# Phasor table, scans and log-decay sums of an S5 and gated-linear-attention mixer

## The chip, the cores and the metric

The kernel runs on one core of a Trainium2 chip, in one launch. The metric is the device time of an execution in microseconds (us). A core has TensorE (matrix products; PE in the rows), VectorE (DVE), ScalarE (ACT), GpSimd (POOL) and SyncE (SP), which here issues the DMAs. Each engine takes its instructions in order and waits on semaphores for the others.

## The reference

A two-layer encoder over 512 tokens of width 1024, float32. The first layer's mixer is what the change touches. Its input projection feeds two branches:

```python
# S5, 32 groups of 16 channels, 64 complex states, both directions
a = exp(lam_re*dt) * (cos(lam_im*dt) + i sin(lam_im*dt))
x = u @ Bbar ; h[t] = a*h[t-1] + x[t]           # reverse for direction 1
y = Re(C h) + D u ; y = gelu(y) ; y = y*sigmoid(y @ glu_w + glu_b)

# GLA, 4 heads, both directions, chunks of 64 tokens
log_a = log_sigmoid(lr @ gate_w + gate_b) / 16
bc = cumsum(log_a within a chunk) ; b_last = bc[:, :, -1]
qd, kd, kc = q*exp(bc), k*exp(-bc), k*exp(b_last - bc)
o = (mask * (qd kd^T)) v + qd S_prev ; S = S*exp(b_last) + kc^T v
```

The branches are concatenated, projected, added and normalized, and a mixture of experts follows. The second layer has windowed attention with a sink logit per head, and again a mixture of experts.

## The kernel before

The S5 branch works in chunks of 8 tokens: products with precomputed matrices do what lies inside a chunk, and a scan goes over the 64 chunks. There are four blocks, two halves of the groups (`hf`) by two directions (`d`); I call them first to fourth in their order of work (first half forward and backward, then second half). A block has:

- `s5_cs`: the phasor table `CS` on GpSimd, powers 0 to 63 of the phase of `a` for 16 groups of states, by doubling: each of five rounds squares the phase (line 653 on the tile `ph`, 128x16) and multiplies the known part of the table by it (six operations). The tag `cs` has two buffers, so the third table waits until the first block has been worked off.
- `s5_x`: the chunk inputs come from TensorE through ScalarE's copies `xb` (709, 710) and are turned by the table on VectorE (722 to 724). Since the phase is taken out, the scan's factor is the real magnitude in `eph`: 16 scans of 128x64 in line 728.
- `s5_back`: TensorE swaps real and imaginary rows (`swap`), VectorE turns the phase back (741 to 743).
- `s5_table` builds `PB` and `Mo` (611 to 613, on VectorE but for the last block's `Mo`, on GpSimd).

Per half, `s5_hs` transposes `HT` on TensorE; ScalarE copies it to `Hs` (760); SyncE writes it to DRAM (`E`) and reads it back as `Mi` with eight DMAs, and `s5_y` forms the output from `Mi`, `Mo` and `XS`, with the gelu in `yg` (791). In SyncE's queue there follow `snk` (the sink logits for the second layer), the router's small weights, four `x` loads and `glw`, the weight of the GLU, which ScalarE rounds to `glh` (801).

In the GLA branch (`gla_a`), heads lie along the free dimension and both directions' 64 features on the partitions. The gate comes from TensorE; the log-sigmoid is min(z,0) minus log(1+exp(-|z|)) (871 to 875). Then eight scans of 64x512, with a factor that is 0 where a chunk begins (879, 880), give the sums within chunks; `bl` (884, 885) is a chunk's last sum; three exponentials on ScalarE (891, 894, 895) and three products (897; two of them on GpSimd) give `kc`, `q2` and `kd`. `gla_b` transposes `kc` to `kcp` (920) and steps the states `St` (934, 938: 56 steps of 64x128 on VectorE), then forms the output.

After the GLU, `mixer0_out` loads the output weight `wo` in two DMAs (988), and the expert weights follow in SyncE's queue (1219).

GpSimd keeps the order of the program. The order of the other engines in the first mixer is set at build time by a scheduler that simulates the program, so that a changed operation moves others.

Of the kernel before, what the change touches and what calls it, by code (L numbers as in the profile page):

```python
# [108 lines left out]
class Net:  # L109
# [64 lines left out]
    def mixer0(self, A, B1):  # L174
# [160 lines left out]
        def lowrank():  # L335
# [311 lines left out]
    def s5_cs(self, d, hf):  # L647

        G, a8 = self.nc.gpsimd, self.a8
        g0 = 32 * d + 16 * hf  # L650

        def tt(o, x, y, op):
            G.tensor_tensor(o, x, y, op=op)
        CS = a8([2, 16, 64], f"CS{d}{hf}", "cs")
        self.CS[d, hf] = CS
        c, s = CS[:, 0], CS[:, 1]
        pc, psn = self.eph[:, 0, g0:g0 + 16], self.eph[:, 1, g0:g0 + 16]
        G.tensor_copy(c[:, :, 1:2], pc[:, :, None])
        G.memset(c[:, :, 0:1], 1.0)
        G.memset(s[:, :, 0:1], 0.0)  # L660
        G.tensor_copy(s[:, :, 1:2], psn[:, :, None])
        ph = a8([23, 16], "ph", "ph")
        tb = a8([16, 32], "phb", "phb")
        cur = (pc, psn)
        m = 2
        while m < 64:
            q = 2 * (m.bit_length() % 2)
            nr, ni = ph[:, q], ph[:, q + 1]

            tt(nr, cur[0], cur[0], OP.mult)  # L670
            tt(ph[:, 4], cur[1], cur[1], OP.mult)
            tt(nr, nr, ph[:, 4], OP.subtract)
            tt(ni, cur[0], cur[1], OP.mult)
            tt(ni, ni, ni, OP.add)
            cur = (nr, ni)
            bs = [128, 16, m]
            mc, ms = (t[:, :, None].to_broadcast(bs) for t in cur)
            t_ = tb[:, :, :m]
            tt(c[:, :, m:2 * m], c[:, :, :m], mc, OP.mult)
            tt(t_, s[:, :, :m], ms, OP.mult)  # L680
            tt(c[:, :, m:2 * m], c[:, :, m:2 * m], t_, OP.subtract)
            tt(s[:, :, m:2 * m], s[:, :, :m], mc, OP.mult)
            tt(t_, c[:, :, :m], ms, OP.mult)
            tt(s[:, :, m:2 * m], s[:, :, m:2 * m], t_, OP.add)
# [143 lines left out]
    def gla_a(self, qk, lrT):  # L828
# [7 lines left out]
        def tile8(name, tag):  # L836
            return self.a8([4, 512], name, tag)
        gt4 = tile8("gt4", "wl")
        WG = gt4[:, 0].rearrange("p (h d e) -> p h d e", h=4, d=2)
        rs = gt4[:, 2]  # L840
        V.memset(WG, 0.0)
        gb = self.small([4], "gb")
        for d in range(2):
# [2 lines left out]
            nc.sync.dma_start(gb[64 * d:64 * d + 64], i["gla_gate_b"][0, d].rearrange("(h e) -> e h", h=4))
        V.memset(rs, 1.0)
        V.memset(rs[0:64].rearrange("p (n c) -> p n c", c=64)[:, :, 0:1], 0.0)
        V.memset(rs[64:128].rearrange("p (n c) -> p n c", c=64)[:, :, 63:64], 0.0)
# [18 lines left out]
        for h in range(4):
            b = self.bank("p")
            self.mm(b, WG[:, h].rearrange("p d e -> p (d e)"), lrT)  # L870
            V.tensor_scalar(la[:, h], b, gb[:, h:h + 1], 0.0, op0=OP.add, op1=OP.min)
            S.activation(lt[:, h], b, AF.Abs, bias=gb[:, h:h + 1])
# [9 lines left out]
        bl = self.small([32], "bl")
        bcv = bc.rearrange("p h (n c) -> p (h n) c", c=64)
        V.tensor_copy(bl[0:64, :, None], bcv[0:64, :, 63:64])
        V.tensor_copy(bl[64:128, :, None], bcv[64:128, :, 0:1])
        dec = self.small([32], "dec", z=5)
        kc = la
        V.tensor_tensor(kc.rearrange("p h (n c) -> p (h n) c", c=64), bl[:, :, None].to_broadcast([128, 32, 64]), bcv,
                        op=OP.subtract)
        S.activation(dec, bl, AF.Exp, scale=1.0 / 16)  # L890
        S.activation(kc, kc, AF.Exp, scale=1.0 / 16)
        kd = tile8("kd", "wh")
        eb = kd
        S.activation(eb, bc, AF.Exp, scale=1.0 / 16)
        S.activation(bc, bc, AF.Exp, scale=-1.0 / 16)
        for nm, o, x, y in (("kc", kc, kc, k2), ("q2", q2, q2, eb), ("kd", kd, k2, bc)):
            (G if nm in ("q2", "kd") else V).tensor_tensor(o, x, y, op=OP.mult)
# [1194 lines left out]
```

## Time and profile before

| | us |
|---|---|
| median of 3 runs (1600.93 to 1603.47) | 1601.02 |
| profiled execution | 1606.41 |
| its span, first to last instruction | 1604.6 |
| PE busy in the span | 1388.4 (87%) |
| DVE busy | 694.6 (43%) |
| ACT busy | 355.6 (22%) |
| POOL busy (385 instructions) | 317.1 (20%) |

The busy shares are means over the whole program, of which the first mixer is the first fifth; the rest is mostly TensorE and weight traffic. So the rows below are by stage. In them a start is counted from the start of the span, and what stands in brackets is the idle time of the engine before the instruction, with what ended it.

### The profile page before, as it was taken

Reading aid. Unit: us, or ns where it says so; the run is one execution under the profiler, and the core shown is the slowest. Engines: PE = TensorE matmul, PEld = TensorE weight load, DVE = VectorE, ACT = ScalarE, POOL = GpSimd, SP = SyncE. Lnnn points to the kernel's source line nnn. Section 1 sums busy time; section 2 is a strip of 40 time slices with the busy share of each in tenths; the row PEclk is TensorE's granted clock in tenths of the full one; section 3 lists DMA queues with packets and bytes.
Section 4 is the critical chain, followed back from the end, with each engine's and each line's share of the span. In section 5 each row is a group of like instructions: output and inputs, shape, how many; then the busy total and the mean of one; then the engine's idle time right before and its main releaser. Section 6 shows DMA issues by size and latency. Waiting matters only on the chain.

```text
span 1604.6 us, 20785 instructions
## 1 busy us (share of the span) xinstructions
PE 1388.4 (87%) x8043; PEld 803.8 (50%) x8043; DVE 694.6 (43%) x1409; ACT 355.6 (22%) x643; POOL 317.1 (20%) x385
## 2 busy tenths in 40 slices
PE   6889726798997999988878898998997999989785
PEld 5778615577552435524324785667342553524242
DVE  8947997556132132311214557865231222311115
ACT  2233612331110101101002366641110110101012
POOL 5996932323000000000001434112000000000003
PEclk9999957798999999999989999998999999999998
DMA  8223006426599999999999116356899999999993
GB/s 183 67 80 86 16 20 184 156 110 240 228 407 423 423 423 424 422 420 423 420 421 358 47 60 186 115 220 242 357 407 422 422 425 422 423 421 422 422 416 132
DMA packets 122695, 461.07 MB, mean 287 GB/s; under 512 B 34650, under 2 KB 60730, under 8 KB 79968
## 3 DMA queue, kind: packets, MB, share of 16 engines
q1 hardware_dynamic: 122480, 459.59, 73.3%
q8 instruction: 65, 1.06, 0.3%
q14 instruction: 38, 0.31, 0.1%
q0 software_dynamic: 112, 0.10, 0.0%
HBM read 454.94 MB, written 4.72 MB: 286 GB/s over the span
## 4 chain that ended last, share of the span: by engine, by line
PE 49%; DMA 24%; DVE 3%; POOL 1%; issue 1%; ACT 1%; SPq 0%; POOLq 0%; ACTq 0%; DVEq 0%
PE b L119 47%; DMA w<-in_moe_w_dram 23%; PE b L133 1%; PE b L1943 1%; DVE x L1085 1%; DVE x L1120 0%; DMA cwo<-in_c_w_out_dram 0%; DVE x L1101 0%; POOL lnmv L1109 0%; DMA bias<-Ld 0%; POOL lnmv L1110 0%; DVE scv L1937 0%; DVE scv L1920 0%; POOL x L1118 0%; POOL lnmv L1073 0%
## 5 line engine op out<-in xcount | busy, mean ns | idle before, releaser
L119 PE MATMUL b<-w,xe 128*64 128x512 f32 (+1 forms) x2144 | 393.6, 614 | 30.5 <-DMA w<-in_moe_w_dram 27.3
L119 PE MATMUL b<-w,hT 128*64 128x512 f32 (+1 forms) x1088 | 227.5, 644 | 38.9 <-DMA w<-in_moe_w_dram 36.0
L119 PEld LDWEIGHTS b<-w,xe 128*64 128x64 f32 (+1 forms) x2144 | 114.7, 127 | 278.8 <-issue 220.7
L1102 POOL TENSOR_SCALAR lnmv<-lnmv 128x1 f32<-128x1 f32 x8 | 3.2, 399 | 960.9 <-DVE x L1101 483.2
L1565 DVE TENSOR_TENSOR x<-x,b 128x512 f32<-128x512 f32 x176 | 112.2, 682 | 143.2 <-PE b L119 140.9
L119 PEld LDWEIGHTS b<-w,hT 128*64 128x64 f32 (+1 forms) x1088 | 61.3, 131 | 190.8 <-issue 111.7
L1535 DVE SCALAR_TENSOR_TENSOR yl<-b,gs,yh 128x512 fp32r<-128x512 f32 x52 | 39.0, 751 | 230.4 <-ACT yh L1534 229.9
L119 PE MATMUL b<-S,xh 128*128 128x256 f32 x448 | 112.2, 291 | 0.0
L119 PE MATMUL b<-S,xl 128*128 128x256 f32 x448 | 110.6, 288 | 0.0
L1512 DVE TENSOR_TENSOR hs<-hs,b 128x512 f32<-128x512 f32 x26 | 17.9, 688 | 202.7 <-PE b L119 202.7
L119 PEld LDWEIGHTS b<-S,xh 128*128 128x128 f32 x448 | 87.3, 195 | 10.0 <-issue 9.9
L1534 ACT ACTIVATE yh<-b,gs 128x512 fp32r<-128x512 f32 x52 | 35.8, 688 | 249.3 <-PE b L119 249.1
L119 PE MATMUL b<-yh,GT 128*128 128x512 f32 x208 | 89.2, 433 | 0.1
L119 PEld LDWEIGHTS b<-S,xl 128*128 128x128 f32 x448 | 87.3, 195 | 0.0
L119 PE MATMUL b<-yl,GT 128*128 128x512 f32 x208 | 81.7, 397 | 0.7 <-DVE yl L1535 0.6
L1520 ACT ACTIVATE hT<-b 128x512 f32<-128x512 f32 x26 | 15.5, 598 | 299.8 <-PE b L133 299.8
L119 PEld LDWEIGHTS b<-yh,GT 128*128 128x128 f32 x208 | 39.5, 190 | 46.1 <-issue 33.8
L119 PE MATMUL b<-wh,xt 128*128 128x256 f32 x384 | 55.8, 298 | 7.1 <-ACT wh L168 4.6
L1511 ACT ACTIVATE hs<-b 128x512 f32<-128x512 f32 x26 | 15.6, 599 | 192.2 <-PE b L119 192.2
L119 PEld LDWEIGHTS b<-wh,xt 128*128 128x128 f32 x384 | 51.4, 204 | 8.2 <-ACT wh L168 5.2
L119 PE MATMUL b<-xTh,spa 128*128 128x512 f32 x160 | 51.6, 393 | 0.5 <-ACT scv L1840 0.5
L1465 ACT ACTIVATE xe<-b 128x512 f32<-128x512 f32 (+1 forms) x56 | 31.8, 568 | 87.4 <-PE b L119 87.4
(411 smaller groups left out, 2245.6 us busy)
## 6 DMA issues: line engine op xcount, KB each, us to landing
w<-in_moe_w_dram SPq DMA_DIRECT2D x288, 1024.0 KB, 19.6
w<-in_moe_w_dram SPq DMA_DIRECT2D x46, 2048.0 KB, 18.8
bias<-Ld SPq DMA_DIRECT2D x32, 384.0 KB, 3.5
wr<-in_ab_w_in_dram SPq DMA_DIRECT2D x8, 1024.0 KB, 6.5
x<-in_x_dram SPq DMA_DIRECT2D x8, 512.0 KB, 6.4
wo<-in_ab_w_out_dram SPq DMA_DIRECT2D x2, 2048.0 KB, 9.3
cw<-in_c_w_in_dram SPq DMA_DIRECT2D x2, 2048.0 KB, 9.4
cwo<-in_c_w_out_dram SPq DMA_DIRECT2D x16, 256.0 KB, 5.2
```

What stands on the lines that cost most here:

```text
L119: self.nc.tensor.matmul(o, l, r, start=start, stop=stop)
L133: self.nc.tensor.transpose(o, i, self.ident[:k, :k])
L1085: V.scalar_tensor_tensor(x, x, mv[:, 2:3], gb[1][:, c], op0=OP.mult, op1=OP.add)
L1102: G.tensor_scalar(mv[:, 3:4], mv[:, 0:1], mv[:, 1:2], -1.0 / 1024, op0=OP.add, op1=OP.mult)
L1465: nc.scalar.activation(xe[:, 2 * kk:2 * kk + 2, 0:n], b.rearrange("p (j s) -> p j s", j=2)[:, :, 0:n], AF.Copy)
L1511: nc.scalar.activation(hs, b1, AF.Silu)
L1512: nc.vector.tensor_mul(hs, hs, b3)
L1520: self.nc.scalar.activation(hT, b.rearrange("p (k s) -> p k s", k=4), AF.Copy)
L1534: nc.scalar.activation(yh[:, j], b[j], AF.Copy, scale=gs)
L1535: nc.vector.scalar_tensor_tensor(yl[:, j], b[j], gs, yh[:, j].bitcast(F32), op0=OP.mult, op1=OP.subtract)
L1565: V.tensor_add(xs, xs, b)
L1943: nc.tensor.transpose(b[:, 128 * g:128 * g + 128], s[:, g, 128 * j:128 * j + 128], self.rev)
```

## The change

- The phasor table is doubled from the first power on, with both planes (real and imaginary) in one operation of 4 dimensions: 24 operations a block in place of 59. The start column is copied by ScalarE, and its two memsets are VectorE's.
- The 16 scans of a block become two of 128x512. Their factor is written by ScalarE to a PSUM bank (two operations of 128x512 a block), and VectorE zeroes it where a group begins.
- The gate is computed with tokens on the partitions, with the bias as a further row of the product. The chunk sums and the remainders to the chunk's end are 64 products of `la` with masks on TensorE, into PSUM; ScalarE takes the exponentials from there, head by head, and VectorE forms `kc`, `q2` and `kd`, head by head. The GLA scans, `bl` and the difference (888) are gone, and GpSimd has none of the products.
- The negation of `snk` goes from VectorE to GpSimd.

```diff
+            V.memset(lrT[32:33], 1.0)
...
     def s5_cs(self, d, hf):
-        G, a8 = self.nc.gpsimd, self.a8
+        G, S, a8 = self.nc.gpsimd, self.nc.scalar, self.a8
...
+        self.nc.vector.memset(CS[:, 0, :, 0:1], 1.0)
+        self.nc.vector.memset(CS[:, 1, :, 0:1], 0.0)
+        S.activation(CS[:, :, :, 1:2], self.eph[:, 0:2, g0:g0 + 16][:, :, :, None], AF.Copy)
+        tb = a8([2, 16, 31], "phb", "phb")
+        m = 1
         while m < 64:
...
+            k = min(m, 63 - m)
+            o, x, bs = CS[:, :, :, m + 1:m + k + 1], CS[:, :, :, 1:k + 1], [128, 2, 16, k]
+            c, w = (CS[:, r:r + 1, :, m:m + 1].to_broadcast(bs) for r in range(2))
+            t_ = tb[:, :, :, :k]
+            G.tensor_tensor(o, x, c, op=OP.mult)
+            G.tensor_tensor(t_, x[:, ::-1], w, op=OP.mult)
+            G.tensor_tensor(o[:, 0], o[:, 0], t_[:, 0], op=OP.subtract)
+            G.tensor_tensor(o[:, 1], o[:, 1], t_[:, 1], op=OP.add)
             m *= 2
...
-        for g in range(16):
-            x1 = XF[:, g] if d == 0 else XF[:, g, ::-1]
-            V.tensor_tensor_scan(x1, self.eph[:, 2, g0 + g:g0 + g + 1].to_broadcast([128, 64]), x1, 0.0,
-                                 op0=OP.mult, op1=OP.add)
+
+        for h in range(2):
+            mg = self.bank().rearrange("p (g n) -> p g n", g=8)
+            S.activation(mg, self.eph[:, 2, g0 + 8 * h:g0 + 8 * h + 8][:, :, None].to_broadcast([128, 8, 64]), AF.Copy)
+            V.memset(mg[:, :, z0:z0 + 1], 0.0)
+            x1, mg = XS[:, h].rearrange("p j n -> p (j n)"), mg.rearrange("p g n -> p (g n)")
+            if d:
+                x1, mg = x1[:, ::-1], mg[:, ::-1]
+            V.tensor_tensor_scan(x1, mg, x1, 0.0, op0=OP.mult, op1=OP.add)
...
+            nc.sync.dma_start(WG[32:33, :, d, :], i["gla_gate_b"][0, d].rearrange("(h e) -> h e", h=4)[None])
+
+        mk = gt4[:, 1].rearrange("p (m i) -> p m i", m=4)
+        for j, op in enumerate((OP.is_ge, OP.is_le, OP.is_lt, OP.is_gt)):
+            V.tensor_scalar(mk[:, j], self.jp, 0.0, None, op0=op)
+        V.memset(mk[0:64, :, 64:128], 0.0)
+        V.memset(mk[64:128, :, 0:64], 0.0)
...
+        zs = []
+        for t in range(4):
+            b = self.bank("p" if t < 2 else "b")
+            self.mm(b, lrT[:, 128 * t:128 * t + 128], gt4[:, 0])
+            S.activation(lt[:, t], b, AF.Abs)
+            zs.append(b)
         S.activation(lt, lt, AF.Exp, scale=-1.0)
         S.activation(lt, lt, AF.Ln, bias=1.0)
-        V.tensor_tensor(la, la, lt, op=OP.subtract)
+        for t in range(4):
+            V.scalar_tensor_tensor(la[:, t], zs[t], 0.0, lt[:, t], op0=OP.min, op1=OP.subtract)
         yield
...
+        kc, kd = lt, tile8("kd", "wh")
         for h in range(4):
...
+            bs = []
+            for m in range(2):
+                b = self.bank("p")
+                for t in range(4):
+                    for d in range(2):
+                        o = 128 * h + 64 * d
+                        self.mm(b[64 * d:64 * d + 64, 128 * t:128 * t + 128], la[:, t, o:o + 64], mk[:, 2 * m + d])
+                bs.append(b)
+            b, r = bs
+            S.activation(kd[:, h], b, AF.Exp, scale=-1.0 / 16)
+            S.activation(b, b, AF.Exp, scale=1.0 / 16)
+            S.activation(kc[:, h], r, AF.Exp, scale=1.0 / 16)
+            for d in range(2):
+                a, c = slice(64 * d, 64 * d + 64), 63 - 63 * d
+                S.activation(dec[a, 8 * h:8 * h + 8, None], b[a].rearrange("p (n c) -> p n c", c=64)[:, :, c:c + 1], AF.Copy)
+            V.tensor_tensor(kc[:, h], kc[:, h], k2[:, h], op=OP.mult)
+            V.tensor_tensor(q2[:, h], q2[:, h], b, op=OP.mult)
+            V.tensor_tensor(kd[:, h], kd[:, h], k2[:, h], op=OP.mult)
...
-        V.tensor_scalar(self.snk[:, 1], self.snk[:, 0], -1.0, None, op0=OP.mult)
+        G.tensor_scalar(self.snk[:, 1], self.snk[:, 0], -1.0, None, op0=OP.mult)
```

The order of the engines changes with it, at three places of the first mixer. On VectorE the third block's scans (728) and the fourth block's turning (722, 723) stood thus before, with the GLA's scans (879, 880) between:

```order
L724 TENSOR_TENSOR XS<-XS,xb_1927 128x4x2x63
L728 SCALAR_TENSOR_TENSOR XS<-eph,XS 128x64 x16
L875 TENSOR_TENSOR la<-la,lt 128x2048
L722 TENSOR_TENSOR XS<-b_2027,CS_1445 128x4x2x63
L723 TENSOR_TENSOR xb_2003<-b_2028,CS_1445 128x8x63
L879 SCALAR_TENSOR_TENSOR lt<-gt_1992,la 64x512
L722 TENSOR_TENSOR XS<-b_2040,CS_1445 128x4x2x63
L880 SCALAR_TENSOR_TENSOR lt<-gt_1992,la 64x512
L879 SCALAR_TENSOR_TENSOR lt<-gt_1992,la 64x512
```

Now there is, from the third block's two scans (716) to the fourth's (`b_1874` to `b_1888` are its inputs, 712 the zeroing of the factor):

```order
L707 TENSOR_TENSOR XS<-XS,xb_1780 128x4x2x63
L716 SCALAR_TENSOR_TENSOR XS<-b_1829,XS 128x512
L716 SCALAR_TENSOR_TENSOR XS<-b_1833,XS 128x512
L705 TENSOR_TENSOR XS<-b_1874,CS_1339 128x4x2x63
L706 TENSOR_TENSOR xb_1850<-b_1875,CS_1339 128x8x63
L705 TENSOR_TENSOR XS<-b_1887,CS_1339 128x4x2x63
L706 TENSOR_TENSOR xb_1851<-b_1888,CS_1339 128x8x63
L712 MEMSET b_1900 128x8
L707 TENSOR_TENSOR XS<-XS,xb_1850 128x4x2x63
L712 MEMSET b_1904 128x8
L707 TENSOR_TENSOR XS<-XS,xb_1851 128x4x2x63
L716 SCALAR_TENSOR_TENSOR XS<-b_1900,XS 128x512
```

The GLA's work no longer stands between the blocks.

On ScalarE, from the second `Hs` copy on, the kernel before has (`kcp`, `kd` and `lt` belong to the GLA, `glh` and `yg` to the end of the S5 branch):

```order
L760 ACTIVATE Hs_2123<-b_2130 128x256
L920 ACTIVATE kcp<-b_2194 128x512
L920 ACTIVATE kcp<-b_2200 128x512
L920 ACTIVATE kcp<-b_2206 128x512
L920 ACTIVATE kcp<-b_2212 128x512
L894 ACTIVATE kd<-lt 128x2048
L895 ACTIVATE lt<-lt 128x2048
L801 ACTIVATE glh<-glw 128x1024 x2
L791 ACT_TABLE_LOAD
L791 ACTIVATE yg_2320<-b_2321 128x4x8x16
L791 ACTIVATE yg_2320<-b_2347 128x4x8x16
```

The changed kernel has, from `glh` on (880 is the Exp into `kd`, 881 the one in place, 882 the one into `kc`, whose buffer is `lt`; `b_2085` and `b_2094` are the sums of head 3):

```order
L788 ACTIVATE glh<-glw 128x1024 x2
L880 ACTIVATE kd<-b_2085 128x512
L881 ACTIVATE b_2085<-b_2085 128x512
L778 ACT_TABLE_LOAD
L778 ACTIVATE yg_2243<-b_2244 128x4x8x16
L882 ACT_TABLE_LOAD
L882 ACTIVATE lt<-b_2094 128x512
L885 ACTIVATE dec<-b_2085 64x8 x2
L778 ACT_TABLE_LOAD
L778 ACTIVATE yg_2243<-b_2270 128x4x8x16
L911 ACTIVATE kcp<-b_2117 128x512
L911 ACTIVATE kcp<-b_2123 128x512
```

The `kcp` copies have moved from ahead of `glh` to behind it, and with them three exponentials and table loads between.

On TensorE, where the products with `Mi` began before:

```order
L119 MATMUL b_2224<-v,kcp 128x128
L119 MATMUL b_2225<-v,kcp 128x128
L119 MATMUL b_2248<-v,kcp 128x128 x4
L119 MATMUL b_2321<-Mi_2139,U 64x128 x2
L119 MATMUL b_2321<-Mo_1773,XS 64x128
L119 MATMUL b_2347<-Mi_2139,U 64x128 x2
L119 MATMUL b_2347<-Mo_1773,XS 64x128
```

The changed kernel has there (`gt,la` are the mask products, 8 to a bank; `b_2007` is head 0, `b_2033` and `b_2042` head 1, `b_2059` and `b_2068` head 2):

```order
L119 MATMUL b_2033<-gt_1837,la 64x128 x2
L119 MATMUL b_2244<-Mi_1977,U 64x128 x2
L119 MATMUL b_2244<-Mo_1626,XS 64x128 x2
L119 MATMUL b_2244<-Mo_1986,XS 64x128
L119 MATMUL b_2270<-Mi_1977,U 64x128 x2
L119 MATMUL b_2270<-Mo_1626,XS 64x128 x2
L119 MATMUL b_2270<-Mo_1986,XS 64x128
L119 MATMUL b_2042<-gt_1837,la 64x128 x8
L119 MATMUL b_2244<-Mo_1986,XS 64x128
L119 MATMUL b_2244<-Mi_1977,U 64x128 x2
L119 MATMUL b_2244<-Mo_1626,XS 64x128 x2
L119 MATMUL b_2244<-Mo_1986,XS 64x128 x2
```

The products of the states (`v,kcp`), which stood ahead of `Mi`, come later, and mask products of heads 1 to 3 stand behind it.

## Rows read from the trace of the kernel before

**Rows 1.** 20-us window: PE, PEld, DVE, ACT, POOL busy (count), PEclk, DMA share, GB/s.

```profile
200.00:220.00 20.00, 0.00 (x0) 0.00 (x0) 19.93 (x11) 0.00 (x0) 16.44 (x6) 0.50 0.00 0
```

**Rows 2.** List of waits, 100 to 330 us: total, times, longest.

```profile
PE b L119 <- DVE XS L728: 30.9, 1, 30.9
ACT dec L890 <- DVE bl L885: 27.0, 1, 27.0
```

**Rows 3.** VectorE's timeline: start, us, engine, line, operation, tiles [idle <-releaser].

```profile
112.62 7.82 DVE L728 TENSOR_TENSOR_SCAN XS<-eph,XS 128x64 f32<-128x64 f32 x16
...
178.59 2.06 DVE L871 TENSOR_SCALAR la<-b,gb 128x512 f32<-128x512 f32 x3
...
187.18 0.67 DVE L722 TENSOR_TENSOR XS<-b,CS 128x504 f32<-128x504 f32 x1
...
191.29 10.13 DVE L728 TENSOR_TENSOR_SCAN XS<-eph,XS 128x64 f32<-128x64 f32 x16
201.35 4.05 DVE L875 TENSOR_TENSOR la<-la,lt 128x2048 f32<-128x2048 f32 x1
...
214.47 3.21 DVE L880 TENSOR_TENSOR_SCAN lt<-gt,la 64x512 f32<-64x512 f32 x1
217.69 1.22 DVE L879 TENSOR_TENSOR_SCAN lt<-gt,la 64x512 f32<-64x512 f32 x1
...
228.53 1.56 DVE L728 TENSOR_TENSOR_SCAN XS<-eph,XS 128x64 f32<-128x64 f32 x8
...
232.81 0.68 DVE L741 TENSOR_TENSOR CS<-b,CS 128x512 f32<-128x512 f32 x1
...
246.51 4.75 DVE L1846 TENSOR_SCALAR snk<-snk 128x16 f32<-128x16 f32 x1 [4.10 <-DMA snk<-in_c_sink_dram]
...
276.74 0.34 DVE L934 SCALAR_TENSOR_TENSOR St<-St,dec,b 64x128 f32<-64x128 f32 x1
277.11 0.35 DVE L938 SCALAR_TENSOR_TENSOR St<-St,dec,b 64x128 f32<-64x128 f32 x1
```

**Rows 4.** GpSimd's timeline (same columns): second, third and fourth table, then `Mo`.

```profile
100.50 0.25 POOL L653 TENSOR_TENSOR CS<-CS,ph 128x32 f32<-128x32 f32 x1
...
115.86 1.05 POOL L653 TENSOR_TENSOR CS<-CS,ph 128x512 f32<-128x512 f32 x1
...
117.99 1.30 POOL L653 TENSOR_TENSOR CS<-CS,phb 128x512 f32<-128x512 f32 x1
...
135.50 0.21 POOL L658 COPY CS<-eph 128x16 f32<-128x16 f32 x1 [12.86 <-DVE XS L743]
...
166.43 0.22 POOL L658 COPY CS<-eph 128x16 f32<-128x16 f32 x1 [2.11 <-DVE XS L743]
...
199.27 2.00 POOL L611 TENSOR_TENSOR Mo<-C,AA 128x1024 f32<-128x1024 f32 x1
```

**Rows 5.** TensorE's timeline: first `HT` transposes, first `Mi` product, last GLU product.

```profile
121.48 0.88 PE L133 MATMUL b<-ident,HT 128*128 128x128 f32 x3 [4.97 <-DVE HT L753]
...
246.30 0.70 PE L119 MATMUL b<-Mi,U 128*64 128x128 f32 x4 [5.83 <-DMA snk<-in_c_sink_dram]
...
303.64 0.39 PE L119 MATMUL b<-glh,yTl 128*128 128x512 f32 x1
```

**Rows 6.** ScalarE's timeline: table load and Exp, second `Hs` copy, `glh`, `yg`.

```profile
188.00 1.28 ACT L873 ACT_TABLE_LOAD   x1
189.29 1.91 ACT L873 ACTIVATE lt<-lt 128x2048 f32<-128x2048 f32 x1
...
234.98 0.39 ACT L760 ACTIVATE Hs<-b 128x256 f32<-128x256 f32 x1 [0.44 <-PE b L133]
...
257.43 2.00 ACT L801 ACTIVATE glh<-glw 128x1024 fp32r<-128x1024 f32 x2 [14.64 <-DMA glw<-in_s_glu_w_dram]
...
262.52 0.60 ACT L791 ACTIVATE yg<-b 128x512 f32<-128x512 f32 x1 [1.79 <-PE b L119]
```

**Rows 7.** SyncE's queue: the issue of `glw`.

```profile
247.46 0.69 SPq L391 DMA_DIRECT2D glw<-in_s_glu_w_dram  x1
```

More of the change, by code (lines that the diff above doesn't have):

```diff
@@ L647, in s5_cs @@
     def s5_cs(self, d, hf):
-        G, a8 = self.nc.gpsimd, self.a8
+        G, S, a8 = self.nc.gpsimd, self.nc.scalar, self.a8
         g0 = 32 * d + 16 * hf
-        def tt(o, x, y, op):
-            G.tensor_tensor(o, x, y, op=op)
         CS = a8([2, 16, 64], f"CS{d}{hf}", "cs")
         self.CS[d, hf] = CS
[L656 to L665, printed above, removed]
-        while m < 64:
[L667 to L684, printed above, removed]
+        self.nc.vector.memset(CS[:, 0, :, 0:1], 1.0)
[3 more added lines that the diff above has]
+        m = 1
+        while m < 64:
+            k = min(m, 63 - m)
[6 more added lines that the diff above has]
+            G.tensor_tensor(o[:, 1], o[:, 1], t_[:, 1], op=OP.add)
             m *= 2
@@ L724, in s5_x @@
             V.tensor_tensor(xv[:, js, :, hi], xv[:, js, :, hi], tmp[:, :, :, hi], op=OP.add)
-        XF = XS.rearrange("p h j n -> p (h j) n")
-        for g in range(16):
-            x1 = XF[:, g] if d == 0 else XF[:, g, ::-1]
-            V.tensor_tensor_scan(x1, self.eph[:, 2, g0 + g:g0 + g + 1].to_broadcast([128, 64]), x1, 0.0,
-                                 op0=OP.mult, op1=OP.add)
+        for h in range(2):
[6 more added lines that the diff above has]
+            V.tensor_tensor_scan(x1, mg, x1, 0.0, op0=OP.mult, op1=OP.add)
     def s5_back(self, d, hf):
@@ L839, in gla_a @@
         WG = gt4[:, 0].rearrange("p (h d e) -> p h d e", h=4, d=2)
-        rs = gt4[:, 2]
         V.memset(WG, 0.0)
-        gb = self.small([4], "gb")
         for d in range(2):
@@ L845, in gla_a @@
             nc.sync.dma_start(WG[16 * d:16 * d + 16, :, d, :], gw)
[L846 to L849, printed above, removed]
+            nc.sync.dma_start(WG[32:33, :, d, :], i["gla_gate_b"][0, d].rearrange("(h e) -> h e", h=4)[None])
[4 more added lines that the diff above has]
+        V.memset(mk[64:128, :, 0:64], 0.0)
         yield
@@ L867, in gla_a @@
         la, lt = tile8("la", "xtA"), tile8("lt", "xtA")
[L868 to L872, printed above, removed]
+        zs = []
[4 more added lines that the diff above has]
+            zs.append(b)
@@ L873, in gla_a @@
         S.activation(lt, lt, AF.Exp, scale=-1.0)
         S.activation(lt, lt, AF.Ln, bias=1.0)
-        V.tensor_tensor(la, la, lt, op=OP.subtract)
+        for t in range(4):
+            V.scalar_tensor_tensor(la[:, t], zs[t], 0.0, lt[:, t], op0=OP.min, op1=OP.subtract)
         yield
-        bc = lt
+        dec = self.small([32], "dec", z=5)
+        kc, kd = lt, tile8("kd", "wh")
         for h in range(4):
-            V.tensor_tensor_scan(bc[0:64, h], rs[0:64], la[0:64, h], 0.0, op0=OP.mult, op1=OP.add)
-            V.tensor_tensor_scan(bc[64:128, h, ::-1], rs[64:128, ::-1], la[64:128, h, ::-1], 0.0,
-                                 op0=OP.mult, op1=OP.add)
@@ L882, in gla_a @@
[L882 to L897, printed above, removed]
+            bs = []
[6 more added lines that the diff above has]
+                bs.append(b)
```

## The prediction

> **What bounds the kernel now.** I read the chain of waits first: it cannot be followed back beyond 320 us, so the first mixer has to be read by stage. The table of 20-us windows shows the stage that matters: from 200 to 220 us TensorE does nothing at all and ScalarE does nothing, while VectorE is busy for 19.93 us with eleven instructions and GpSimd for 16.44 [rows 1]. The list of waits names the same hole twice: TensorE waits 30.9 us, once, for the S5 scans of line 728, and ScalarE 27.0 us for `bl`, which follows the GLA scans [rows 2]. Then I read VectorE's rows through that hole. Sixteen scans of 128x64 took 10.13 us beside GpSimd's phasor table; eight of the same took 1.56 with GpSimd idle. A 64x512 scan of the decays took 3.21 beside GpSimd and 1.22 alone [rows 3]. So the stage is bound by VectorE, and part of that by the company of GpSimd. Behind it the chain runs over the last S5 half (swap on TensorE, `Hs` on ScalarE, a round trip through DRAM to `Mi`), the GLA states (the `St` rows), GLU, and the copy of `wo`; from there the weight stream of the first MoE hangs on the place where SyncE gets to it, and I let every microsecond won before pass through 1:1.
>
> **S5 scans: 16 of 128x64 become 2 of 128x512.** The trace has no 128x512 scan with a multiplicand in PSUM. The nearest rows are the 64x512 scans: 1.22 alone, 3.21 beside GpSimd [rows 3]. I take 1.22: VectorE's multiplies with one operand in PSUM took 0.67 beside the table and 0.68 with GpSimd idle, so an operand from PSUM takes the contention away [rows 3]. The Trainium skill says the same ("SBUF — State Buffer", section "Who interferes with whom"): a VectorE instruction with at most one input in SBUF does not contend with GpSimd; by this rule the new scan costs 1.22 beside a table too, and without it 3.21. The trace agrees for multiplies and shows no such scan.
> A block's scans then cost 2.44 instead of 7.82, 10.13 or 3.12. In the first block TensorE idles 4.97 us at 121.48 for `HT`, which stands behind these scans on VectorE [rows 3, 5]; 7.82 - 2.44 = 5.4 covers it, so this wait goes: 5.0 us. The two multiplicands a block are written by ScalarE (0.6 us each by the `yg` row of 128x512 [rows 6]) while it waits anyway, and cost nothing; if that cover were gone, 1.2 us a block.
>
> **Phasor table: 59 GpSimd operations a block become 24.** GpSimd's multiplies took 0.25 at 32 elements, 1.05 at 512 and 2.00 at 1024; its add and subtract 1.30 at 512 [rows 4]. On a line through these, the twelve multiplies (32 to 992 elements, 1984 in each of two sets) cost 2 x (6 x 0.20 + 1984 x 0.00175) = 9.3 us, the twelve subtracts and adds (16 to 496) 2 x (6 x 0.20 + 992 x 0.00215) = 6.7: 16 a block. That is the low end; the high end is no gain, as the strided two-plane operands have no row. Now the fourth table runs from 166.43 to the start of the `Mo` work at 199.27 [rows 4], 32.8 us. Its start hangs on the buffer that the block two before frees: the third table waited 12.86 us for it [rows 4]. Both buffers come free some 5 us earlier, and the third table is shorter, so I put the fourth at 157 to 174 and the `Mo` work behind it (17.3 us now) to 189. On GpSimd nothing else waits: the gain is that the table is out of VectorE's way. ScalarE's copy of the start column stands in its queue ahead of each table; I price it at nothing, as GpSimd waits for the buffer then.
>
> **Decay sums on TensorE.** The third S5 block started at 187.18. TensorE's 5.0 carry over to it, and the bias operations of line 871 (2.06 for three, some 2.7 for four) no longer stand before it: 179.6. Its multiplies (187.18 to 191.29) cost 4.1 as before, the scans 2.4: 186.1, against 201.35. Before, the subtraction of line 875 (4.05) and the decay scans now pushed the fourth block's scans back to 230.09; now they come straight behind: 4.1 + 2.4 more, 192.6. From there to the end of the second `Hs` copy it took 5.3 (230.09 to 235.37 [rows 3, 6]). In the new order that copy stands behind a table load and an Exp on ScalarE, 1.28 + 1.91 [rows 6]: 201.1, or 34 us earlier. Then a load and Ln, and four small operations of 0.67 on VectorE, give `la` at 207.0; the 64 mask products come on a TensorE that is idle, except those that stand behind `Mi`.
>
> **What is late next.** The second `Hs` copy starts SyncE's chain E, `Mi`, the small loads and `glw`. Now `glw` was issued 12.1 us after the copy's end and landed another 9.96 later, where `glh` on ScalarE waits for it [rows 6, 7]. I keep these 22.1: `glw` lands at 223.2. This is the new wait. In the old order only `glh` and work that was not urgent stood there; in the new one the exponentials of head 3 stand behind `glh` in ScalarE's queue, and all of the `kcp` copies behind them, on which the GLA states hang. By then they wait: `Mi` came 10.9 us after the copy's end (TensorE goes on at 246.30 [rows 5]), so at 212, and the mask products of heads 1 to 3, which stand behind it on TensorE, are through by some 220. Then, with durations of rows 6: `glh` 2.0, two Exp 1.2, load 1.28, `yg` 0.6, load 1.28, Exp 0.6, the two `dec` copies some 0.5, load 1.28, `yg` 0.6, four `kcp` copies 2.1: 11.4, 234.6; the first products after them let `St` start at 235.9. Its 56 steps follow each other by 0.37 (the last two rows' spacing, [rows 3]): 20.7, with the two `gll` operations 2.3 and 1.5 for waits between: 260.5. Before, the last ended at 277.46 (277.11 + 0.35). The difference is **17 us**. That `snk` leaves VectorE's queue is inside this: there VectorE waited 4.10 us for its DMA and then spent up to 4.75 on it, among the `St` steps [rows 3].
> The Trainium skill speaks against the change here ("ScalarE: Activation LUTs", section "What ACT_TABLE_LOAD costs"): a switch of the table set is 1.28 us of load and 1.38 of drain. Here the Exp starts 0.01 us behind the end of the load at 188.00 [rows 6]: no drain is to be seen. By the page the three loads on this piece would cost 4.1 us more, and the gain would be 13.
>
> **Sum.** The profiled execution took 1606.41 us (1604.6 of span and 1.8 around it); 17 less is 1589.4. It lies 5.4 above the median of the runs, 1601.02, which I take off: **1584 us**. The forecast's own range, with waits in the ScalarE chain a few us either way, is 1577 to 1590.
>
> **Rivals.**
> *GpSimd stays slow* (0.18). Small or strided operations cost what they cost now, the fourth table takes its 32.8 us and ends at 190, `Mo` at 207, and the four late scans run beside it at 3.21. Each block is 4 us later, `Hs` 8. For it: the table's price has no row. Against: the first operands come from PSUM. Gain 9: 1592.
> *The new wait isn't there* (0.16). If `glw` lands before ScalarE gets to it, 5 us of the wait go, and a TensorE that pauses less may keep its clock: it was granted 0.50 (the 1.2 GHz level) in the idle window [rows 1], and the work behind `Mi` ran at this level; 5 more. Gain 27: 1574. Against: `glw` hangs on the same copy as `Mi`.
> *The new wait decides* (0.10): slower. In the new order `St`'s end is `Hs`'s end plus 59.4 (22.1 + 12.7 + 24.6), while the old one didn't hang on `glw`. So the change gains only if the second `Hs` copy ends before 218.1, 17.3 us earlier than now; if the banks that the fourth block borrows, or the multiplicands from ScalarE, hold the S5 blocks where they were, all of the removed work on VectorE is lost in this queue: up to 17 us slower, 1618; half as bad, 1609. For it: one queue decides. Against: ten of the 34 us are removed by scans alone, and nothing that holds the block is on the list of waits.
> *The change doesn't reach the end* (0.04): the weight stream of the first MoE is set by something earlier, 1601. Against: SyncE issues it behind `wo`, whose buffer waits for the GLU.
>
> **How the numbers follow.** Forecast 0.52, the rivals 0.18, 0.16, 0.10, 0.04. Range 1569 to 1599: forecast and the first two rivals with some room, 0.86 of the cases less what may fall outside them. Faster by over 0.2% (3.2 us, about what a measurement of this kernel can tell from no change): 0.84; within 0.2%: 0.06; slower: 0.10.
>
> **What would show it.** In the profile after: scans of 128x512 near 1.2 us even where GpSimd is busy; a GpSimd table of about 16 us; no idle of TensorE before the `HT` transposes of the first half; the second `Hs` copy near 201; `glh` still waiting for `glw`, with the exponentials of the last head behind it; no `snk` among the `St` rows; the last `St` near 260 and the last GLU product near 287 instead of 304 [rows 5]. Scans of 3 us, or a `Hs` copy later than 218, would make the forecast wrong; so would a `St` chain that starts much later than 13 us after `glw`.

## The result, and the profile after

The changed kernel takes 1625.43 us (median, 1624.78 to 1626.93), the kernel before on the same chip 1600.97: ratio 1.0153 [1.0135, 1.0171], **slower by 24 us**, where 1584 was forecast. Its profiled execution took 1625.35 us, its span 1623.6. The loss is there at the last GLU product, 19.8 us later than before; what follows is equally long (1299.8 us of span, before 1300.6). The profiled execution of the kernel before was 5.4 us slower than its median, so the two spans differ by 19.0 us only. VectorE is busy for 675.9 us and GpSimd for 273.5 (244 instructions), both less than before, and TensorE for 1410.8, more.

| us from the span's start | before | forecast | after |
|---|---|---|---|
| third block starts | 187.18 | 179.6 | 201.16 |
| second `Hs` copy ends | 235.37 | 201.1 | 222.41 |
| `glw` landed, `glh` starts | 257.43 | 223.2 | 246.78 |
| first `St` starts | 241.32 | 235.9 | 264.40 |
| last `St` ends | 277.46 | 260.5 | 292.95 |
| last GLU product ends | 304.03 | 287 | 323.85 |

The hole of [rows 1] is gone, as this window row shows (TensorE and ScalarE work in it, VectorE is not full):

```profile
200.00:220.00 20.00, 13.56 (x67) 8.93 (x68) 17.29 (x29) 6.07 (x11) 3.41 (x2) 0.74 0.01 4
```

What was lost lies on both sides of it. First, VectorE's timeline of the changed kernel: the first block's `HT`, a scan beside the third table, and the way into the third block (start, us, engine, line, operation, tiles):

```profile
118.90 2.34 DVE L716 TENSOR_TENSOR_SCAN XS<-b,XS 128x512 f32<-128x512 f32 x2
121.16 0.20 DVE L738 TENSOR_TENSOR HT<-HT 128x64 f32<-128x64 f32 x1
121.40 0.67 DVE L740 SCALAR_TENSOR_TENSOR HT<-eye,Dv,HT 128x16 f32<-128x16 f32 x4
...
146.48 2.34 DVE L716 TENSOR_TENSOR_SCAN XS<-b,XS 128x512 f32<-128x512 f32 x2
...
178.98 2.86 DVE L614 TENSOR_TENSOR PB<-PB,TPB 128x1024 f32<-128x1024 f32 x1
...
181.77 2.92 DVE L614 TENSOR_TENSOR PB<-PB,TPB 128x1024 f32<-128x1024 f32 x1
184.61 4.25 DVE L613 TENSOR_TENSOR TMo<-C,AA 128x1024 f32<-128x1024 f32 x2
...
189.92 2.04 DVE L738 TENSOR_TENSOR HT<-HT 128x64 f32<-128x64 f32 x1
191.88 3.04 DVE L614 TENSOR_TENSOR Mo<-Mo,TMo 128x1024 f32<-128x1024 f32 x1
194.85 6.39 DVE L740 SCALAR_TENSOR_TENSOR HT<-eye,Dv,HT 128x16 f32<-128x16 f32 x4
201.16 0.67 DVE L705 TENSOR_TENSOR XS<-b,CS 128x504 f32<-128x504 f32 x1
...
204.92 2.34 DVE L716 TENSOR_TENSOR_SCAN XS<-b,XS 128x512 f32<-128x512 f32 x2
```

And GpSimd's: a multiply of the third table, then the end of the fourth and the `Mo` work behind it:

```profile
146.86 1.11 POOL L664 TENSOR_TENSOR CS<-CS 128x512 f32<-128x512 f32 x1
...
178.01 2.75 POOL L664 TENSOR_TENSOR CS<-CS 128x992 f32<-128x992 f32 x1
180.73 2.88 POOL L665 TENSOR_TENSOR phb<-CS 128x992 f32<-128x992 f32 x1
183.69 2.00 POOL L666 TENSOR_TENSOR CS<-CS,phb 128x496 f32<-128x496 f32 x1
...
189.29 2.58 POOL L612 TENSOR_TENSOR Mo<-C,AA 128x1024 f32<-128x1024 f32 x1 [1.51 <-ACT xb L693]
191.84 2.00 POOL L613 TENSOR_TENSOR TMo<-C,AA 128x1024 f32<-128x1024 f32 x1
193.92 3.20 POOL L614 TENSOR_TENSOR Mo<-Mo,TMo 128x1024 f32<-128x1024 f32 x1
197.09 2.00 POOL L612 TENSOR_TENSOR Mo<-C,AA 128x1024 f32<-128x1024 f32 x1
```

The kernel before had the same two VectorE operations on `PB` in its own line 613, and the four small ones on `HT` in line 753, beside smaller operations of GpSimd:

```profile
176.31 1.20 DVE L613 TENSOR_TENSOR PB<-PB,TPB 128x1024 f32<-128x1024 f32 x1
177.44 1.23 DVE L613 TENSOR_TENSOR PB<-PB,TPB 128x1024 f32<-128x1024 f32 x1
...
185.93 0.66 DVE L753 SCALAR_TENSOR_TENSOR HT<-eye,Dv,HT 128x16 f32<-128x16 f32 x4
```

```profile
175.22 4.00 POOL L653 TENSOR_TENSOR ph<-ph 128x16 f32<-128x16 f32 x5
```

Read starts and durations of both engines against each other: a VectorE operation with two operands in SBUF and a GpSimd operation take turns, and a row's time holds the wait for the other engine. `PB` from 178.98 ends at 181.84, 1.1 us behind the GpSimd multiply that ends at 180.76; the next multiply, begun at 180.73, ends at 183.61, 1.8 behind `PB`. So a 1.2-us operation takes 2.9 beside one of 992 elements. Four operations of 16 elements, 0.67 us in all at 121.40, take 6.39 at 194.85. What these stand beside is not the table but GpSimd's `Mo` work: it is as large as before, but the table ends at 187.77 instead of 199.27, so this work has moved up beside `HT`. The scans, with an operand in PSUM, take 2.34 for two, and so they do at 146.48 beside a multiply of the third table: that step of the forecast held.

ScalarE's timeline from the second `Hs` copy to the last `kcp` ([rows 6] are those of before):

```profile
222.05 0.36 ACT L747 ACTIVATE Hs<-b 128x256 f32<-128x256 f32 x1
...
246.78 2.00 ACT L788 ACTIVATE glh<-glw 128x1024 fp32r<-128x1024 f32 x2 [4.47 <-DMA glw<-in_s_glu_w_dram]
248.80 0.60 ACT L880 ACTIVATE kd<-b 128x512 f32<-128x512 f32 x1
...
249.91 1.28 ACT L778 ACT_TABLE_LOAD   x1
...
253.11 0.60 ACT L882 ACTIVATE lt<-b 128x512 f32<-128x512 f32 x1
...
256.68 1.08 ACT L911 ACTIVATE kcp<-b 128x512 f32<-128x512 f32 x2 [0.83 <-PE b L133]
...
262.27 0.60 ACT L911 ACTIVATE kcp<-b 128x512 f32<-128x512 f32 x1 [2.59 <-PE b L133]
```

The queue is as forecast, `glh` waiting for `glw` with head 3's exponentials and all of `kcp` behind it. But the four `kcp` copies take 6.2 us instead of 2.1 (256.68 to 262.87), the last with 2.59 us of wait for its transposes, and `St` starts 17.6 us after `glh` instead of 12.7. TensorE's rows of these transposes (between them stand products `q,kd` of the GLA; the products with `Mi` are over by 246.5):

```profile
253.76 0.90 PE L133 MATMUL b<-ident,lt 128*128 128x128 f32 x3 [6.33 <-ACT lt L882]
...
258.98 2.67 PE L119 MATMUL b<-q,kd 64*128 64x128 f32 x18
261.58 0.66 PE L133 MATMUL b<-ident,lt 128*128 128x128 f32 x4
```

Then VectorE's and TensorE's timelines and the window row of the states:

```profile
264.40 0.34 DVE L925 SCALAR_TENSOR_TENSOR St<-St,dec,b 64x128 f32<-64x128 f32 x1 [1.18 <-PE b L119]
...
274.05 0.35 DVE L929 SCALAR_TENSOR_TENSOR St<-St,dec,b 64x128 f32<-64x128 f32 x1 [1.84 <-PE b L119]
...
292.60 0.35 DVE L929 SCALAR_TENSOR_TENSOR St<-St,dec,b 64x128 f32<-64x128 f32 x1
```

```profile
271.97 3.06 PE L119 MATMUL b<-v,kcp 64*128 64x128 f32 x16 [5.42 <-DVE St L925]
...
288.66 0.70 PE L119 MATMUL b<-St,q 128*64 128x128 f32 x4
...
323.46 0.39 PE L119 MATMUL b<-glh,yTl 128*128 128x512 f32 x1
```

```profile
280.00:300.00 20.00, 16.06 (x76) 10.95 (x75) 12.21 (x31) 1.36 (x11) 0.00 (x0) 0.50 0.00 1
```

TensorE and VectorE wait for each other by turns until 288 us, up to 5.42 us at a time on the one side and three times 1.84 on the other, and TensorE's granted clock in the window is 0.50, the 1.2 GHz level.

### The profile page after: what moved, and what is told of

It reads as the page before. It is cut to its first block, busy times and chain, and to the rows that moved or that the text cites. A ratio compares the mean times of both kernels' runs of the same rounds, so it can differ in the third digit from the quotient of the medians.

```text
span 1623.6 us, 20890 instructions
## 1 busy us (share of the span) xinstructions
PE 1410.8 (87%) x8171; PEld 822.8 (51%) x8171; DVE 675.9 (42%) x1371; ACT 364.9 (22%) x673; POOL 273.5 (17%) x244
## 5 line engine op out<-in xcount | busy, mean ns | idle before, releaser
L119 PE MATMUL b<-w,hT 128*64 128x512 f32 (+1 forms) x1088 | 224.0, 651 | 34.6 <-DMA w<-in_moe_w_dram 31.8
L1525 ACT ACTIVATE yh<-b,gs 128x512 fp32r<-128x512 f32 x52 | 35.7, 687 | 241.7 <-PE b L119 241.4
## 6 DMA issues: line engine op xcount, KB each, us to landing
w<-in_moe_w_dram SPq DMA_DIRECT2D x288, 1024.0 KB, 19.8
```

The lines of the kernel that those rows point to most:

```text
L119: self.nc.tensor.matmul(o, l, r, start=start, stop=stop)
L1525: nc.scalar.activation(yh[:, j], b[j], AF.Copy, scale=gs)
```

## The experiments

Shown are the marks of one profiled execution each; its own time lies up to 6 us from the median. "Rest" is the span less the last GLU product. The experiments ran on four chips (e1 to e4, e5 to e8, f, g); each ratio is to the kernel before on the same chip, where its median was 1603.27, 1601.91, 1602.51 and 1603.16. So runs of different groups are compared here by their ratios, and a difference of medians between them can be some us off.

| | median | ratio to before | `Hs` end | `St` | GLU end | rest |
|---|---|---|---|---|---|---|
| before | 1600.97 | 1 | 235.4 | 241.3 to 277.5 | 304.0 | 1300.6 |
| after | 1625.43 | 1.0153 [1.0135, 1.0171] | 222.4 | 264.4 to 293.0 | 323.9 | 1299.8 |
| e1 | 1602.96 | 1.0002 [0.9980, 1.0025] | 231.8 | 242.5 to 273.4 | 297.1 | 1299.1 |
| e2 | 1607.53 | 1.0019 [1.0005, 1.0033] | 226.8 | 239.2 to 270.9 | 301.0 | 1300.2 |
| e3 | 1622.37 | 1.0108 [1.0078, 1.0139] | 224.7 | 267.8 to 296.5 | 326.6 | 1293.2 |
| e4 | 1610.16 | 1.0029 [1.0014, 1.0044] | 214.3 | 257.3 to 286.0 | 316.2 | 1290.3 |
| e5 | 1598.42 | 0.9986 [0.9967, 1.0004] | 234.5 | 245.1 to 272.4 | 296.1 | 1300.4 |
| e6 | 1597.71 | 0.9965 [0.9948, 0.9983] | 213.2 | 244.0 to 272.6 | 303.6 | 1287.7 |
| e7 | 1612.89 | 1.0061 [1.0041, 1.0081] | 223.6 | 254.7 to 281.5 | 312.0 | 1300.2 |
| e8 | 1621.72 | 1.0108 [1.0078, 1.0138] | 218.9 | 262.4 to 291.0 | 321.3 | 1299.8 |
| f1 | 1583.19 | 0.9881 [0.9861, 0.9901] | 214.8 | 241.1 to 261.5 | 287.6 | 1292.6 |
| f2 | 1592.43 | 0.9941 [0.9924, 0.9958] | 214.6 | 241.4 to 270.0 | 301.4 | 1290.8 |
| f3 | 1581.28 | 0.9872 [0.9851, 0.9892] | 212.0 | 237.9 to 258.3 | 284.4 | 1291.1 |
| f4 | 1599.40 | 0.9975 [0.9962, 0.9988] | 223.0 | 249.3 to 269.7 | 295.8 | 1301.9 |
| g1 | 1590.28 | 0.9916 [0.9893, 0.9938] | 214.0 | 240.0 to 260.4 | 290.7 | 1297.6 |
| g2 | 1589.49 | 0.9919 [0.9892, 0.9946] | 223.1 | 249.4 to 269.8 | 295.9 | 1291.5 |
| g3 | 1597.39 | 0.9951 [0.9931, 0.9971] | 234.3 | 244.8 to 275.5 | 302.1 | 1293.5 |

**One part alone, or all but one.** These take hunks of the change's diff as they stand there: e1 is before with the new `s5_cs`, e2 before with the scans of `s5_x`, e3 before with the new `gla_a`, e4 the changed kernel with the old `s5_cs`; e1 needs room for its scratch tile besides, for which two small tiles move (first cut below), and e5 is before with one line (second cut):

```diff
+        self.bl = gt4[:, 1, 0:32]
...
-        gb = self.small([4], "gb")
+        gb = gt4[:, 3, 0:4]
...
-        bl = self.small([32], "bl")
+        bl = self.bl
```

```diff
-        V.tensor_scalar(self.snk[:, 1], self.snk[:, 0], -1.0, None, op0=OP.mult)
+        G.tensor_scalar(self.snk[:, 1], self.snk[:, 0], -1.0, None, op0=OP.mult)
```

> The kernel before with the new phasor table alone (24 GpSimd operations, start column on ScalarE; two small tiles share another tile's space). Theory A, the larger GpSimd operations of the new table hold up VectorE's operations with two SBUF inputs: the PB and Mo operations beside the first and fourth table take 2 to 3 us each instead of 1.2, the third block starts 8 to 14 us later, and the time rises by 6 to 15 us to 1607 to 1616. Theory B, the loss is in the order behind glw and the table is as harmless as its busy time says: the time stays within 3 us of 1601 or falls by up to 5. Theory C, lower granted clock of TensorE alone: within 3 us of 1601.

> The kernel before with the two scans of 128x512 a block alone. All theories: a scan takes 1.2 us beside the table too (2.34 for two in the changed kernel), the first block's 5 us and the third block's 7.5 us of scans go. Theory A: 8 to 13 us faster, 1588 to 1593, as nothing else on VectorE is slowed. Theory B: the same or less, at least 4 us faster. A rival that the gain is hidden by the decay scans that follow: within 3 us of 1601.

> The kernel before with the decay sums on TensorE alone (old table, old scans). Theory A: VectorE loses 20 us of work between the third and the fourth block, the second Hs copy comes 10 to 20 us earlier; the new wait behind glw takes most back: between 8 us faster and 3 us slower, 1593 to 1604. Theory B, the order (exponentials of head 3 behind glh, then the states in lockstep with TensorE at the low clock) is what costs: 8 to 25 us slower, 1609 to 1626.

> The changed kernel with the old table of 59 small operations. Theory A: the third block starts at about 186 instead of 201 us, the second Hs copy ends near 208, and by the rule that the end follows this copy the time falls by 12 to 20 us, to 1605 to 1613. Theory B: the third block may start earlier but the time stays within 4 us of 1625, as the wait behind glw decides. Theory C, clock alone: within 4 us of 1625.

> The kernel before with the negation of snk on GpSimd alone. All theories: the stall of VectorE between two St steps goes (4.10 us of wait and up to 4.75 of the operation). If the St steps are what the end hangs on there: 4 to 8 us faster, 1595 to 1599 against 1603. Rival: the St steps then wait for TensorE's products instead, and the time stays within 3 us.

The GLA alone brings the whole delay of the GLU (+22.6 in e3), though its `Hs` copy ends 10.7 us earlier than before. With the old table in the changed kernel (e4) the third block starts at 180.83 instead of 201.16. But its fourth block then waits 7.03 and 2.65 us for that longer table, so the `Hs` copy is 8.1 us earlier and the GLU 7.6; what e4 gains beyond that lies behind the GLU (see the place of `wo`). So the table costs something in this company. In the old one (e1) no loss can be told, though 6 to 15 us were expected: its stretched `PB` rows are there too, and the third block starts 11.5 us later, but the GLA scans come after GpSimd is done:

```profile
177.54 2.86 DVE L613 TENSOR_TENSOR PB<-PB,TPB 128x1024 f32<-128x1024 f32 x1
...
211.64 1.22 DVE L863 TENSOR_TENSOR_SCAN lt<-gt,la 64x512 f32<-64x512 f32 x1
```

In e2 it is the reverse: the S5 scans are short and the third block starts 8.7 us earlier, so the GLA scans move in beside GpSimd's `Mo`, and a part of the gain is lost there. The `Hs` copy is still 8.6 us earlier, but the first `St` only 2.1, as VectorE waits 3.35 us for the DMA of `snk` ahead of it. The time is 0.2% longer, where 8 to 13 us less were expected; where the last 3 us of the gain went, its profiled execution, the fastest of ten, doesn't show:

```profile
203.41 3.20 DVE L883 TENSOR_TENSOR_SCAN lt<-gt,la 64x512 f32<-64x512 f32 x1
...
219.75 2.34 DVE L733 TENSOR_TENSOR_SCAN XS<-b,XS 128x512 f32<-128x512 f32 x2
```

In e5 the last `St` is 5 us earlier, but its time can't be told from that of before.

**The queue on ScalarE.** e6 (from e4) and e7 (from the changed kernel) let ScalarE issue `glh` and the second half's `yg` only behind the last `kcp` copy:

```diff
+            with self.tc.issue_after(self.kcp_last.ins):
                 S.activation(gh[:, k], glw[:, k], AF.Copy)
```

> The changed kernel with the old table, and with glh and the second half's yg held behind the kcp copies in ScalarE's queue. Theory B (the wait for glw ahead of head 3's exponentials, and the three table loads, hold the states back): the last kcp copy comes 10 to 15 us earlier than the 253.6 of the old-table run, the first St step at 241 to 247 instead of 257.3, and the time falls by 8 to 16 us to 1594 to 1602, faster than the kernel before or equal to it. Rival, the states are held by TensorE at the low clock and by their own lockstep with it: St starts earlier but the end moves by less than 4 us, 1606 to 1614.

> The changed kernel (new table) with glh and the second half's yg held behind the kcp copies. Theory B: 8 to 16 us faster than the changed kernel, 1609 to 1617; what is left over the kernel before is the new table's. Rival (lockstep and clock): less than 4 us faster, 1621 or more.

By the ratios e6 gains 10 us on e4 and e7 15 on the changed kernel; the GLU ends 12.6 and 11.9 earlier, and `St` starts 13.4 and 9.7 earlier. The place of `kcp` behind `glh` is worth that much.

**The size of GpSimd's operations.** e8 is the changed kernel with the table's operations cut by groups to at most 128 elements:

```diff
-            G.tensor_tensor(o, x, c, op=OP.mult)
+            for g in range(n):
+                e = slice(16 // n * g, 16 // n * (g + 1))
+                G.tensor_tensor(o[:, :, e], x[:, :, e], c[:, :, e], op=OP.mult)
```

> The changed kernel with the new table's operations of over 128 elements a plane pair cut into pieces of at most 128 (54 operations a block instead of 24, the same two-plane form). Theory A as the size of the operation (a VectorE operation with two SBUF inputs waits for one whole GpSimd operation, so small ones cost it little): the PB and Mo operations of the second half take 12 to 14 us together instead of 21, the third block starts near 187 instead of 201, and the time is as with the old table, 1605 to 1614. Rival, the two-plane strided form or the earlier place of the table: PB and Mo still take 18 us or more, the time stays above 1620.

VectorE's rows, then GpSimd's:

```profile
178.01 1.39 DVE L614 TENSOR_TENSOR PB<-PB,TPB 128x1024 f32<-128x1024 f32 x1
...
198.18 0.68 DVE L711 TENSOR_TENSOR XS<-b,CS 128x504 f32<-128x504 f32 x1 [2.33 <-POOL CS L672]
```

```profile
178.40 1.33 POOL L672 TENSOR_TENSOR CS<-CS,phb 128x128 f32<-128x128 f32 x1
...
198.86 0.42 POOL L673 TENSOR_TENSOR CS<-CS,phb 128x124 f32<-128x124 f32 x1
```

`PB` is back at 1.39 us, and the `PB` and `Mo` rows of the second half take 14.0 us instead of 21.1: their stretching is a matter of the size of the other engine's operation. `HT` takes 2.0 us instead of 8.4, as GpSimd's `Mo` work begins only behind it, at 199.24. The third block starts at 189.43 instead of 201.16. But the table now ends at 199.3, the fourth block waits for it, and only 2.6 us of the 11.7 reach the GLU; 1605 to 1614 were expected.

**The states.** f1 (from e6) takes the banks of every other head's state products from another pool, f2 (from e6) issues the `Mi` and `Mo` products only behind the last `kcp` transpose, f3 does both; f4 is e7 with both:

```diff
-            bs = [self.bank("p"), self.bank("p")]
+            bs = [self.bank("b" if h % 2 else "p") for _ in range(2)]
```

```diff
+                        with self.tc.issue_after(self.kcp_tp.ins) if hf else ExitStack():
```

> The old-table, kcp-first kernel with the banks of the state products of heads 1 and 3 taken from the other set, so that TensorE need not wait for a head's St steps before it forms the next head's products. If the lockstep is a cost of its own: the three waits of VectorE of 1.84 us among the St steps and TensorE's 3.9 us waits go, St takes 23 to 25 us instead of 28.6, and the time falls by 3 to 6 us, to 0.993 to 0.995 of the kernel before. Rival, the output products set the end whatever St does: within 2 us of the kcp-first kernel (0.9965).

> The old-table, kcp-first kernel with the products of Mi held behind the transposes for kcp on TensorE, so that the mask products of heads 1 to 3 don't stand behind Mi. If this wait is what is left between the second Hs copy and St: the last kcp copy at 232 to 236 instead of 242.4, St starts 6 to 10 us earlier, and the time falls by 5 to 10 us, to 0.990 to 0.994 of the kernel before. Rival, the products of Mi then come in the way of the output: within 3 us of the kcp-first kernel.

> Both of these together, old table. If the two costs add: 8 to 15 us faster than the kcp-first kernel, 0.987 to 0.992 of the kernel before. If TensorE's low clock over the output products takes it back: 0.993 to 0.997.

> The same two edits and kcp first with the new table of 24 operations. Theory A: the third block stays at 201 us and the end follows it, so this is 10 to 16 us slower than the same with the old table, 0.994 to 1.002 of the kernel before. Rival: in the better order the table no longer matters, within 3 us of the old-table kernel.

By the ratios the banks are worth 13 us (f1) and both edits together 15; f2's order alone is worth 4, which isn't clear of the noise. TensorE's rows and the window of f1:

```profile
239.93 3.39 PE L119 MATMUL b<-v,kcp 64*128 64x128 f32 x48
...
263.36 0.44 PE L119 MATMUL b<-St,q 128*64 128x128 f32 x4
```

```profile
260.00:280.00 20.00, 18.95 (x142) 13.82 (x139) 13.13 (x31) 9.09 (x38) 5.54 (x5) 1.00 0.91 316
```

Of the 64 state products 48 go in one run, the 56 `St` steps take 20.4 us instead of 28.7 (e6), and behind them the clock is granted in full: an output group takes 0.44 instead of 0.70. The edit moved other work as well: the last `kcp` copy ends at 239.1 instead of 242.4, so not all of the 13 us need be the banks'.

**The place of `wo`.** With the old table beside the new GLA the rest is 7 to 12 us shorter (e3, e4, e6, f1 to f3). There the first half of `wo` lies elsewhere in SBUF, and its DMA does not wait for the GLU's operand. g1 is f3 with that wait put back, g2 is f4 and g3 is before without it:

```diff
-        tb = a8([16, 32], "phb", "phb")
+        tb = a8([16, 39], "phb", "phb")
```

```diff
-        zone = dict(tt=0, ht=0, ph=0, phb=0, wlr=0, ...
+        zone = dict(tt=0, ht=0, ph=0, phb=5, wlr=0, ...
```

> f3_both (1581.28) with the old table's scratch tile `phb` lengthened from 32 to 39 columns a group, so that it takes 448 bytes more of its region; no instruction of the first mixer changes or moves up to the GLU. With it the buffer of the first half of wo lies over the GLU's operand, as in the kernels with the new table, and the copy into it has to wait for the last GLU product. Theory (the place of wo): last GLU product at 284.4 as in f3_both, the time behind it 8 to 11 us longer, 1589 to 1592. Rival (the old table's gain is all of it less contention): 1581.

> f4_both_new_table (1599.40) with the new table's scratch tile `phb` in another region of SBUF, so that the first half of wo does not lie over the GLU's operand; VectorE's, ScalarE's, GpSimd's and TensorE's order before the GLU stays, the four x loads move behind wo in SyncE's queue. Theory (the place of wo): last GLU product near 296, the time behind it 8 to 11 us shorter, 1588 to 1592; the 8 us that then still lie between this kernel and f3_both are contention with GpSimd's larger operations. Rival (all contention): 1599.

> The kernel before with its scratch tile `phb` in another region, as in g2. Theory (the place of wo is a matter of its own and was no part of the change's loss, as both kernels wait there): last GLU product at 304, time behind it 8 to 11 us shorter, 1591 to 1594. Rival (only the new order of the GLA's tail can use an earlier wo): 1601 to 1603.

f4 has the wait and g2 not, in ScalarE's rows (one each):

```profile
303.96 3.90 ACT L995 ACTIVATE hi<-wo 128x1024 fp32r<-128x1024 f32 x4 [3.65 <-DMA wo<-in_ab_w_out_dram]
```

```profile
286.70 3.89 ACT L995 ACTIVATE hi<-wo 128x1024 fp32r<-128x1024 f32 x4
```

By the ratios the wait costs 7 us with the old table (f3, g1) and 9 with the new (f4, g2), and g3 won 8, each within some 3 to 5 us; by the medians g3 won 5.8, where 9 to 12 were expected. In g2 and g3 the four `x` loads move behind `wo` in SyncE's queue besides, and in g3 `glh` starts 6.0 us earlier than before. Of g1's later GLU (6.4 us), some 2 were there already at the `Hs` copy; why the clock was lower from 270 to 280 us (0.52, in f3 1.00) in it stays open. With `wo` alike on both sides, the old table is the faster one by some 8 (f3, g2) and 9 us (g1, f4). That this is due to the size of its operations is shown for the `PB` rows (e8), not for all of it. The fastest, f3, is the new scans and the new GLA with the old table and three changes of order: ratio 0.9872 [0.9851, 0.9892].

## Why the prediction was wrong

- **Right:** the scans (1.2 us each, also beside GpSimd), the `HT` wait of TensorE gone, the fourth block straight behind the third, `glh` waiting for `glw` and what stands behind it, `snk` gone from the `St` rows (e5: last `St` 5 us earlier, the time not clear of the noise).
- **The step that failed first:** "the gain is that the table is out of VectorE's way". It rested on the table's sum, 16 us (measured: 19.0 for the third table, 23.1 for the fourth), and on [rows 3, 4] read for the scans alone. The third block's other VectorE work has two operands in SBUF, and its price goes by the length of the GpSimd operations beside it, not by their number or sum; by the forecast's own times GpSimd was busy beside all of it. The `PB` and `Mo` rows of the second half took 21.1 us instead of 12.65, the two `HT` lines 8.4 instead of 1.7 (0.47, and 1.25 up to the third block), these beside GpSimd's `Mo` work, which was to end at 189 and ran from 189.29 to 203.49. The first table did the same earlier: the first block began at 115.18 instead of 107.94, which ate the 5 us that were to carry over (the second block starts at 141.50, before 141.59; in e2, with the old table, at 135.13). 8.5 + 6.7 + 5.9 (the `PB` work at 172.3, 0.9 late instead of 5 early) is 21.1 of the 21.6 us by which the third block is late.
 The Trainium skill has the rule ("SBUF — State Buffer", "Who interferes with whom"): with two inputs in SBUF a VectorE instruction contends with a GpSimd instruction that reads SBUF, and the port pair that they share is an exclusive lock. The rows agree, 2.9 us beside 2.8, and show the turns to be whole instructions. I used its half on one input, for the scans, and not this one for the rest.
- **From the `Hs` copy to the first `St`:** 42.0 instead of 34.8 us: `glw` landed 24.4 after the copy (22.1 assumed), and the four `kcp` copies took 6.2 us instead of 2.1, with their transposes standing among the `q,kd` products on TensorE.
- **States to GLU:** 28.6 and 30.9 us instead of 24.6 and 26.6. I took the old kernel's spacing of the steps and 1.5 us for waits. Steps and products ran in a lockstep over the three banks of their pool, in which VectorE waited three times 1.84 us, 5.5 in all, and behind it TensorE worked with the clock at its lower level. With other banks, and at the full clock, f1 has 20.4 and 26.1 us.

The misses add up: 21.3 + 7.2 + 3.9 + 4.3 = 36.7 us, from 287 to 323.9. By these numbers neither half makes much of a loss alone. With the `Hs` copy in time and the measured tail of 101.4 us, the GLU would have ended at 302.5, a gain of 1.5; with the tail as forecast, at 308.4, a loss of 4.4. The runs give the tail the greater weight: with the old table (e4) the GLU still ends 12.2 us later than before, and with the new table but `kcp` first and the two edits of the states (f4) it ends 8.2 us earlier.

The rival *the new wait decides* had the right side and place, and a chance of 0.10. What held the `Hs` copy was not what it named (banks, factors from ScalarE), and its point of change was too late: with the measured tail the copy had to end before 202.6, not 218.1. *GpSimd stays slow* was wrong in its form: the table did get shorter (fourth: 164.66 to 187.77, 23.1 us) and did harm by it.

## What to carry to other kernels

Fewer and longer GpSimd operations are no relief for VectorE: count which VectorE instructions with two SBUF operands run beside them, and charge each about the length of one GpSimd operation. A shorter table also moves up what stands behind it on its engine: look at what that will run beside. When work is moved behind a DMA wait in an engine's queue, price the whole tail behind it, with its banks and the granted clock, and not with the spacing that it had while nothing waited. When a scratch tile changes size, look at what lies over it later: here that decided 7 to 9 us, and it could have been taken for an effect of the operations.

## What the runs showed of the hardware

- VectorE's operations with two SBUF operands and GpSimd's alternate instruction by instruction: a 128x16 operation of 0.17 us (121.40) took 1.6 (194.85) beside GpSimd operations of 2.00 to 3.20.
- It works the other way too: in the kernel before, GpSimd's 16-element multiplies took 0.8 us each beside VectorE (4.00 for five at 175.22), where five take 1.17 with VectorE idle (102.01).
- In the changed kernel TensorE's clock was at the lower level (0.50) from 270 to 310 us: TensorE was busy for 4.1 and 6.1 us of the first two tens, in pieces between waits, and for all of the next two. In f2 it was low from 264 to 288 us with TensorE busy for all of it. What brings it back isn't settled here.
